# A two-layer encoder trunk: where small constants are fetched, and the order of casts, residual adds and norm operands at the ends of feed-forward and attention

## The chip, the cores and the metric

The kernel runs on one core of a Trainium2 chip. The metric is the device time of one execution in microseconds, the median of several runs. Besides the runs there is one profiled execution, from which all views of the profile come.

The core's engines are named as the profile names them: PE (TensorE, matrix products; PEld is its weight load), DVE (VectorE), ACT (ScalarE), POOL (GpSimd) and SP (SyncE, which here only issues transfers). An engine works through its own queue in order; engines wait for each other by semaphores.

## The reference

Input x has 256 tokens of 1024 float32 values. Each of two layers computes

```
x = x + 1/2 * SwiGLU_1(RMSNorm(x))                     # feed-forward, width 2816
h = RMSNorm(x);  q,k,v = h @ W_in
x = x + concat(windowed_attention_A, differential_attention_B) @ W_out
x = x + 1/2 * SwiGLU_2(RMSNorm(x))
```

and a last RMSNorm gives the output. Every RMSNorm has a learned gain per channel. The attention needs small inputs besides: the gains of the norms, a sink logit per head, four vectors whose products give the lambda of the differential attention, and tables of distances.

## The kernel before

**Precision.** Matrix products are made of three float32r products each. A weight tile lands as `raw` (4 x 128 rows of 512 columns, 1 MB). ACT casts it to `whi`, and DVE subtracts to get the rest, `wlo`. The activations are split in the same way, and each step takes hi x hi, lo x hi and hi x lo. `raw` has 6 buffers, `whi` and `wlo` have 3 each.

**Stream of weights.** All tiles of the whole kernel stand in one list, `specs`, in the order in which they are used. `ahead(n)` (line 198) issues the casts up to tile n and the transfers for which buffers are free; `weights()` (line 219) calls it with two tiles of lookahead and hands out the next tile. The transfers are issued by SP.

**Order of work.** The wrappers `pe`, `act` and `dve` (line 40) keep the program's order while `kept[0]` is true. In `mix`, the attention, it is set to false after the first products (line 780) and to true again before the output projection (line 908); in between a scheduler orders the instructions. POOL is used without a wrapper, so the scheduler may order its instructions throughout.

**A norm** is an instance of `Norm` (line 273). It needs no normalised copy of x: the gain is multiplied into the transposed x, and the row's factor r is applied later to the products.

- `turn(j)` transposes two of eight chunks of x on PE into a bank of PSUM.
- `operands(j)` makes the operand pair j of it. For each of its two chunks, ACT writes gain times x as the high part, and DVE the rest as the low part.
- `squares` sums x squared on ACT. `stats` makes r from the sums, on DVE and POOL.

`make_sums` and `by_seven` belong to another way to multiply, which is off: `SEVEN` is empty, so neither is called.

**Start.** SP fetches the first gain table, and the first tiles of gate and up in four slices of 256 KB each, interleaved; ACT's queue fetches x in four parts. `take_x` (line 381) makes the first norm between the slices: pairs 0 and 1, then 2 and 3, at k == 2 its squares and `stats`. From line 424 on POOL issues eight small transfers of constants (three gain tables, the sinks, the four lambda vectors), the last five broadcast to 128 partitions, then an iota, memsets and small products of them. `attention_constants`, called inside the third column group of the first feed-forward, reads them.

**Feed-forward.** `ffn` goes over five groups of 512 hidden columns and a last one of 256. For each, PE makes gate and up from the norm's operands, ACT and DVE make the hidden values, PE transposes them and adds their product with the down weights into four banks.

**End of a feed-forward** (`ffn_close`, line 688). PE's order is: the products of the last down tiles for the left half of x, written `group(0, ...)`, `tail(0)`; those of the right half, `group(1, ...)` and `tail(1)`, in pieces; between them the transposes for pairs 0 and 1 of the next norm. DVE adds the residual, left half first. The cast of one more weight tile, `ahead(at["use"] + LOOK - 1)`, stands on line 701, behind the pairs and the squares. That tile is the second one used by the next stage. After attention's entry the first products with pairs 0 and 1 run, then `late` makes pairs 2 and 3 from the right half of x.

**End of attention** (from line 841). PE multiplies the values of path B (`osl`, 16 matmuls) and of path A (`oa`, 32 matmuls of 64 columns); the trace has two records for each of these, 32 and 64. `norm_b` (line 858) normalises path B's heads: squares on ACT, sums on DVE, the power on POOL, the product on DVE, eight transposes on PE, and the split with the gain into `oT[2]` and `oT[3]` by ACT and DVE. In the program's text it is called before the last two of the eight (t, c) steps of path A's matmuls. Path A is divided by its sums into `oan` on DVE. Then the output projection runs, first over path B's rows, then over path A's.

Of the kernel before, what the change touches and what calls it, by code (L numbers as in the profile page):

```python
# [34 lines left out]
def trunk(ctx: ExitStack, tc: tile.TileContext, x, n1, g1, u1, d1, nm, w_in, sink,  # L35
          lq1, lk1, lq2, lk2, subln, w_out, n2, g2, u2, d2, nf, out):
    nc = tc.nc
    pool, sp = nc.gpsimd, nc.sync

    class Kept:  # L40


        def __init__(self, eng):
            self.eng = eng
# [26 lines left out]
    def bank():  # L71
        return ps.tile([P, 512], F32, tag="ps", bufs=8, name=nm_("ps"))
# [4 lines left out]
    def blk(dt=F32R):  # L77
        return s4.tile([P, 2, 512], dt, tag="s4", name=nm_("s4"))
# [194 lines left out]
    class Norm:  # L273


        def __init__(self, g0, sums=len(SEVEN) > 0):
            self.g0, self.xs, self.sums = g0, [], sums
            self.xg = []
            self.ss = tmp("nss", 2, (P, 2, 4))

        def squares(self, t, c, n):
# [13 lines left out]
        def operands(self, j, sl):  # L295
            xs = blk()
            self.xs.append(xs)
            for i in range(2):
                g = gcol[:, self.g0 + 2 * j + i:self.g0 + 2 * j + i + 1]
                act.activation(xs[:, i, 0:S], sl[:, i], AF.Identity, scale=g)  # L300
                dve.scalar_tensor_tensor(xs[:, i, S:512], in0=sl[:, i], scalar=g, in1=f(xs[:, i, 0:S]),
                                         op0=ALU.mult, op1=ALU.subtract)
            if self.sums:
                if j % 2 == 0:
                    self.xg.append(blk(F32).rearrange("p a (c s) -> p (a c) s", c=2))
                for i in range(2):
                    act.activation(self.xg[j // 2][:, j % 2 * 2 + i], sl[:, i], AF.Identity,
                                   scale=gcol[:, self.g0 + 2 * j + i:self.g0 + 2 * j + i + 1])

        def make_sums(self):  # L310

            (t0, t1), (b0, b1) = [(t[:, :, 0:P], t[:, :, P:S]) for t in self.xg]
            self.sm = []

            def make(x, y, op):
                v = tmp().rearrange("p a (c s) -> p (a c) s", c=2)
                dve.tensor_tensor(v, x, y, op=op)
# [4 lines left out]
                return v  # L322

            s1 = make(b1, t1, ALU.subtract)
            s2 = make(s1, t0, ALU.add)
            make(t1, t0, ALU.subtract)
            make(b0, s2, ALU.subtract)

        def quarter(self, t, b):

# [50 lines left out]
    def take_x(k):  # L381

        g, u = early
        if k == 0:
            for j in (0, 1):
                sl = norm.turn(j)
                next(g)
                norm.operands(j, sl)
                next(u)
        elif k == 1:  # L390
            for e in (g, u, g, u):
                next(e)
# [12 lines left out]
    grow = const.tile([NG - 16, P], F32, name="grow")  # L405
    distB = const.tile([P, 2, S], F32, name="distB")
# [20 lines left out]
    pool.dma_start(snk_in, sink.rearrange("l h -> (l h)").partition_broadcast(P))  # L427
    for i, a in enumerate((lq1, lk1, lq2, lk2)):
        pool.dma_start(lin[:, i], a.rearrange("l d -> (l d)").partition_broadcast(P))
    pool.iota(dist_i.rearrange("p a b -> p (a b)"), pattern=[[P, 2], [-1, S]], base=0, channel_multiplier=1)  # L430

    for c in range(4):
        pool.memset(qscA[0:64, c:c + 1], -0.125 / slopeA[c])
        pool.memset(qscA[64:128, c:c + 1], -0.125 / slopeA[c + 4])
        pool.memset(qscB[:, c:c + 1], -0.125 / slopeB[c])

    sv = snk_in.rearrange("p (l s c) -> p l c s", l=DEPTH, s=2)
    for t in range(2):
        for l in range(DEPTH):
            pool.tensor_copy(snk[:, l, :, t, :], sv[:, l])  # L440
    pool.tensor_scalar(nsnk.rearrange("p a b c d -> p (a b c d)"), snk.rearrange("p a b c d -> p (a b c d)"),
                       -1.0, 0.0, op0=ALU.mult, op1=ALU.add)
    for i in range(2):
        pool.tensor_tensor(lpr[:, i], lin[:, 2 * i], lin[:, 2 * i + 1], op=ALU.mult)

    def attention_constants():
        gsl = bank()
# [67 lines left out]
    class Residual:  # L515
# [14 lines left out]
        def late(self, k):  # L530

            if k == 1:
                self.nxt.pair(2)
                self.nxt.pair(3)
                self.squares(1)
            elif k == 2:
                self.nxt.stats()
                if self.nxt.sums:
                    self.nxt.make_sums()

    def ffn(norm, aside=None, before=None, final=False):
        def silu(out_, acc, t):
# [95 lines left out]
        tokens(us, norm.xs, weights(), 4)  # L638
        h = hidden(g, us)
        for n in range(1, NGRP):  # L640
            if n == 3 and aside is not None:
# [12 lines left out]
            h = hidden(g, us)  # L654
            for hh in range(2):
                down(hT, n - 1, hh, weights())
# [31 lines left out]
    def ffn_close(parts, nxt):  # L688
        group, tail = ffn_end(parts, (FC - 1, G4 + 3))
        res = Residual(nxt, parts[0])  # L690
        group(1, [(0, t) for t in range(2)])
        tail(0)
        for t in range(2):
            res.add(0, t)
        tail(1)
        group(1, [(1, t) for t in range(2)])
        for j in range(2):
            nxt.pair(j)
        res.squares(0)
        group(1, [(2, t) for t in range(2)])  # L700
        ahead(at["use"] + LOOK - 1)
        group(1, [(3, t) for t in range(2)])
        for t in range(2):
            res.add(1, t)
        nxt.late = res.late

    def mix(l, norm, nxt_norm):
# [150 lines left out]
        def norm_b():  # L858
# [16 lines left out]
            for hp, src in enumerate(turned(on)):  # L875
# [66 lines left out]
    for l in range(DEPTH):  # L942
        final = l == DEPTH - 1
        parts = ffn(norm, attention_constants, take_x) if l == 0 else ffn(norm)
        norm_m = Norm(16 + l * 8, False)
# [77 lines left out]
```

## Time and profile before

| what | value |
|---|---|
| time, median of 3 runs | 976.37 us (976.16 to 978.26) |
| profiled execution, its own time | 975.68 us |
| its span in the profile | 973.9 us |
| instructions | 12341 |
| granted clock of PE, mean | 0.999 |
| PE busy | 956.1 us |
| DVE, ACT, POOL busy | 558.7, 479.0, 20.2 us |
| moved by DMA | 169.38 MB, mean 174 GB/s |

How to read the views. Times run from the span's start. A line in order of time gives the start, the duration, the engine, the line of the code, the operation, what it writes <- what it reads, the shape and how often; in square brackets stands the idle time of the engine before it, and what ended that. Most instructions carry line 50, the wrapper's, so they are told apart by their tiles: `ps` is a bank of PSUM, `s` an operand or hidden block, `ident` the matrix for transposes, `xk` the residual x. A window's line gives its length, the busy time and number of instructions of each engine, the clock and the share of DMA.

### The profile page before, as it was taken

The numbers are of one execution on the slowest core, as the hardware profiler recorded it, in microseconds if no ns is written. First come the engines' busy times: TensorE is split into PE (matmuls) and PEld (weight loads), VectorE is DVE, ScalarE is ACT, GpSimd is POOL, SyncE is SP. The second block draws the span as 40 slices with busy tenths as digits, with TensorE's granted clock in tenths as the row PEclk, the third lists the DMA queues.
The fourth block names the chain that finished last, engine by engine and source line by source line (L and its number), as shares of the span: only waits on it lengthen the run. The fifth ranks groups of instructions, "written<-read, shape, count | busy, mean of one in ns | idle before, by whom it ended". The sixth has DMA issues, their size and how long they took to land.

```text
span 973.9 us, 12341 instructions
## 1 busy us (share of the span) xinstructions
PE 956.1 (98%) x4940; PEld 807.9 (83%) x4940; DVE 558.7 (57%) x854; ACT 479.0 (49%) x781; POOL 20.2 (2%) x49
## 2 busy tenths in 40 slices
PE   8999999999999999999999999999999999999997
PEld 5888888889888888888888888887999788888886
DVE  4745545479846545445465455555796565445553
ACT  4735444368635534444364434435675464434433
POOL 3000000000000000000000000000000000000001
PEclk9999999999999999999999999999999999999999
DMA  9955556545424655556556556554652356565501
GB/s 284 374 200 190 173 176 212 174 147 153 135 66 151 216 199 190 173 180 208 173 173 195 189 183 201 183 173 132 204 156 73 130 173 201 188 204 202 179 1 43
DMA packets 98217, 169.38 MB, mean 174 GB/s; under 512 B 3182, under 2 KB 30896, under 8 KB 98160
## 3 DMA queue, kind: packets, MB, share of 16 engines
q1 hardware_dynamic: 96816, 167.27, 51.8%
q0 software_dynamic: 256, 0.29, 0.4%
q10 hardware_dynamic: 1088, 1.05, 0.3%
q8 instruction: 38, 0.62, 0.3%
q14 instruction: 19, 0.16, 0.0%
HBM read 167.54 MB, written 1.05 MB: 173 GB/s over the span
## 4 chain that ended last, share of the span: by engine, by line
PE 94%; DVE 2%; DMA 1%; ACT 1%; issue 1%; POOLq 0%; POOL 0%; SPq 0%
PE ps L50 94%; DMA raw<-in_ffn_w_gate_dram 1%; DVE s L50 1%; DVE wlo L50 1%; ACT s L50 0%; ACT whi L50 0%; DVE xk L50 0%; DMA xk<-in_x_dram 0%; ACT junk L50 0%; ACT tmp L50 0%; POOLq L1018 0%; POOL rf L968 0%; DVE rf L50 0%; SPq L162 0%
## 5 line engine op out<-in xcount | busy, mean ns | idle before, releaser
L50 PE MATMUL ps<-whi,s 128*128 128x512 f32 (+1 forms) x2316 | 718.3, 391 | 2.8 <-DVE s L50 1.2
L50 DVE TENSOR_TENSOR wlo<-raw,whi 128x1024 fp32r<-128x1024 f32 (+2 forms) x392 | 378.5, 1014 | 229.8 <-ACT whi L50 225.9
L50 PEld LDWEIGHTS ps<-whi,s 128*128 128x128 f32 x2316 | 431.2, 188 | 91.7 <-ACT whi L50 2.3
L50 PE MATMUL ps<-wlo,s 128*128 128x512 f32 x1158 | 450.8, 389 | 0.2 <-DVE wlo L50 0.2
L50 ACT CAST whi<-raw 128x1024 fp32r<-128x1024 f32 (+2 forms) x392 | 323.1, 884 | 244.9 <-PE ps L50 222.0
L50 PEld LDWEIGHTS ps<-wlo,s 128*128 128x128 f32 x1158 | 217.7, 188 | 47.1 <-DVE wlo L50 2.3
L50 PE MATMUL ps<-s,whi 128*128 128x256 f32 x448 | 83.1, 286 | 1.4 <-ACT whi L50 1.4
L50 PEld LDWEIGHTS ps<-s,whi 128*128 128x128 f32 x448 | 70.1, 192 | 2.8 <-ACT whi L50 1.8
L50 ACT CAST s<-ps 128x512 fp32r<-128x512 f32 x48 | 26.0, 589 | 94.2 <-PE ps L50 94.2
L50 DVE TENSOR_TENSOR s<-ps,s 128x512 fp32r<-128x512 f32 x48 | 31.1, 687 | 71.6 <-ACT s L50 71.6
L50 PE MATMUL ps<-s,wlo 128*128 128x256 f32 x224 | 63.5, 284 | 1.5 <-DVE wlo L50 1.5
L50 ACT ACTIVATE tmp<-ps,r 128x512 f32<-128x512 f32 (+1 forms) x48 | 30.8, 654 | 45.6 <-PE ps L50 45.6
L50 DVE SCALAR_TENSOR_TENSOR s<-ps,hr,tmp 128x512 f32<-128x512 f32 (+1 forms) x48 | 32.4, 706 | 31.8 <-PE ps L50 25.4
L50 ACT ACTIVATE s<-ps,gcol 128x256 fp32r<-128x256 f32 x48 | 21.6, 472 | 51.0 <-PE ps L50 33.1
L50 PEld LDWEIGHTS ps<-s,wlo 128*128 128x128 f32 x224 | 42.9, 192 | 1.9 <-DVE wlo L50 1.9
L50 PE MATMUL ps<-ident,s 128*128 128x128 f32 x304 | 39.9, 273 | 0.0
L50 PEld LDWEIGHTS ps<-ident,s 128*128 128x128 f32 x304 | 35.1, 141 | 4.7
L50 DVE SCALAR_TENSOR_TENSOR s<-ps,gcol,s 128x256 fp32r<-128x256 f32 x48 | 22.3, 482 | 28.2 <-ACT s L50 28.2
L50 ACT ACTIVATE s<-s,negm 128x256 f32<-128x256 f32 x64 | 31.9, 500 | 7.4 <-DVE negm L50 7.4
L345 POOL TENSOR_TENSOR r<-ms,mhalf 128x2 f32<-128x2 f32 x6 | 4.2, 702 | 646.1 <-DVE ms L50 646.1
L50 PE MATMUL ps<-ident,xk 128*128 128x128 f32 x96 | 14.5, 288 | 1.9 <-DVE xk L50 1.1
L50 PEld LDWEIGHTS ps<-ident,xk 128*128 128x128 f32 x96 | 11.6, 146 | 4.7 <-DVE xk L50 1.9
(94 smaller groups left out, 274.4 us busy)
## 6 DMA issues: line engine op xcount, KB each, us to landing
raw<-in_ffn_w_down_dram SPq DMA_DIRECT2D x44, 1024.0 KB, 4.9
raw<-in_ffn_w_gate_dram SPq DMA_DIRECT2D x39, 1024.0 KB, 5.0
raw<-in_ffn_w_up_dram SPq DMA_DIRECT2D x39, 1024.0 KB, 5.0
raw<-in_w_in_dram SPq DMA_DIRECT2D x14, 1024.0 KB, 5.0
raw<-in_ffn_w_gate_dram SPq DMA_DIRECT2D x8, 512.0 KB, 3.6
raw<-in_ffn_w_up_dram SPq DMA_DIRECT2D x8, 512.0 KB, 4.6
raw<-in_w_in_dram SPq DMA_DIRECT2D x8, 512.0 KB, 4.5
raw<-in_w_out_dram SPq DMA_DIRECT2D x4, 1024.0 KB, 4.8
```

The source lines that it names most:

```text
L50: ins = issue(*a, **k)
L345: pool.tensor_tensor(self.r, ms, mhalf[:, 0:2], op=ALU.pow)
```

## The change

Five edits:

1. The constants' block becomes a function `constants()`, called in `take_x` at k == 2 behind `stats()`. POOL gets the wrapper, so its program order is kept.
2. In `operands`, both activations are issued first and then both subtractions.
3. In `ffn_close`, the line with `ahead` moves from behind the next norm's pairs and squares to directly behind `tail(1)`.
4. In `mix`, `kept[0] = True` moves up, ahead of path A's matmuls, so that the end of attention, `norm_b` among it, stands in program order.
5. `make_sums` is rewritten and its calls move; as `SEVEN` is empty, it is called neither before nor after.

```diff
-    pe, act, dve = Kept(nc.tensor), Kept(nc.scalar), Kept(nc.vector)
+    pe, act, dve, pool = Kept(nc.tensor), Kept(nc.scalar), Kept(nc.vector), Kept(nc.gpsimd)
...
         def operands(self, j, sl):
             xs = blk()
             self.xs.append(xs)
-            for i in range(2):
-                g = gcol[:, self.g0 + 2 * j + i:self.g0 + 2 * j + i + 1]
+            gs = [gcol[:, self.g0 + 2 * j + i:self.g0 + 2 * j + i + 1] for i in range(2)]
+            for i, g in enumerate(gs):
                 act.activation(xs[:, i, 0:S], sl[:, i], AF.Identity, scale=g)
+            for i, g in enumerate(gs):
                 dve.scalar_tensor_tensor(xs[:, i, S:512], in0=sl[:, i], scalar=g, in1=f(xs[:, i, 0:S]),
                                          op0=ALU.mult, op1=ALU.subtract)
...
             norm.stats()
-            if norm.sums:
-                norm.make_sums()
+            constants()
...
-    for i, g in enumerate((nm, n2)):
-        pool.dma_start(grow[i * 16:(i + 1) * 16], g.rearrange("l (k p) -> (l k) p", p=P))
-    pool.dma_start(grow[32:34], subln)
...
+    def constants():
+        for i, g in enumerate((nm, n2)):
+            pool.dma_start(grow[i * 16:(i + 1) * 16], g.rearrange("l (k p) -> (l k) p", p=P))
+        pool.dma_start(grow[32:34], subln)
+        pool.dma_start(snk_in, sink.rearrange("l h -> (l h)").partition_broadcast(P))
+        for i, a in enumerate((lq1, lk1, lq2, lk2)):
+            pool.dma_start(lin[:, i], a.rearrange("l d -> (l d)").partition_broadcast(P))
+        pool.iota(dist_i.rearrange("p a b -> p (a b)"), pattern=[[P, 2], [-1, S]], base=0, channel_multiplier=1)
...
         tail(1)
+        ahead(at["use"] + LOOK - 1)
         group(1, [(1, t) for t in range(2)])
         for j in range(2):
             nxt.pair(j)
         res.squares(0)
         group(1, [(2, t) for t in range(2)])
-        ahead(at["use"] + LOOK - 1)
         group(1, [(3, t) for t in range(2)])
...
+        kept[0] = True
         oa = [bank() for _ in range(2)]
         for t in range(2):
             for c in range(4):
...
-        kept[0] = True
         w = weights()
```

On the engines' queues the change leaves the number of instructions as it is. On PE, only the eight transposes at each end of attention move: they stand behind 24 of path A's 32 matmuls (48 of 64 records) instead of behind 30, in between the last ones. On DVE at that place, a small instruction of `norm_b` (`dd`) moves behind the sums of squares, and the division of path A (`ra`, `oan`) behind the split of path B. On ACT and DVE at the three ends of `ffn_close`, the two casts and two subtractions of one tile move ahead of the operands of pairs 0 and 1. On POOL, the constants move behind r.

More of the change, by code (lines that the diff above doesn't have):

```diff
@@ L37, in trunk @@
     nc = tc.nc
-    pool, sp = nc.gpsimd, nc.sync
+    sp = nc.sync
     class Kept:
@@ L273, in trunk, with __init__ @@
     class Norm:
-        def __init__(self, g0, sums=len(SEVEN) > 0):
-            self.g0, self.xs, self.sums = g0, [], sums
-            self.xg = []
+        def __init__(self, g0):
+            self.g0, self.xs = g0, []
             self.ss = tmp("nss", 2, (P, 2, 4))
@@ L297, in operands, with make_sums, part, make @@
             self.xs.append(xs)
-            for i in range(2):
-                g = gcol[:, self.g0 + 2 * j + i:self.g0 + 2 * j + i + 1]
+            gs = [gcol[:, self.g0 + 2 * j + i:self.g0 + 2 * j + i + 1] for i in range(2)]
+            for i, g in enumerate(gs):
                 act.activation(xs[:, i, 0:S], sl[:, i], AF.Identity, scale=g)
+            for i, g in enumerate(gs):
                 dve.scalar_tensor_tensor(xs[:, i, S:512], in0=sl[:, i], scalar=g, in1=f(xs[:, i, 0:S]),
                                          op0=ALU.mult, op1=ALU.subtract)
-            if self.sums:
-                if j % 2 == 0:
-                    self.xg.append(blk(F32).rearrange("p a (c s) -> p (a c) s", c=2))
-                for i in range(2):
[L307 to L317, printed above, removed]
+        def make_sums(self):
+            self.sm = []
+            def part(b, t):
+                vs = [f(self.xs[2 * b + i]) for i in range(2)]
+                return [[v[:, :, c + t * P:c + (t + 1) * P] for v in vs] for c in (0, S)]
+            def make(x, y, op, rest):
+                v = tmp().rearrange("p a (c s) -> p (a c) s", c=2)
+                for i in range(2):
+                    vi = v[:, 2 * i:2 * i + 2]
+                    dve.tensor_tensor(vi, x[i], y[i], op=op)
+                    for z, o in rest:
+                        dve.tensor_tensor(vi, vi, z[i], op=o)
                 sm = blk().rearrange("p a (c s) -> p (a c) s", c=2)
@@ L321, in make @@
                 self.sm.append(sm)
[L322 to L327, printed above, removed]
+                return [v[:, 0:2], v[:, 2:4]]
+            add, sub = ALU.add, ALU.subtract
+            (t0h, t0l), (t1h, t1l), (b0h, b0l), (b1h, b1l) = [part(b, t) for b in range(2) for t in range(2)]
+            s1 = make(b1h, t1h, sub, [(b1l, add), (t1l, sub)])
+            s2 = make(s1, t0h, add, [(t0l, add)])
+            make(t1h, t0h, sub, [(t1l, add), (t0l, sub)])
+            make(b0h, s2, sub, [(b0l, add)])
         def quarter(self, t, b):
@@ L423, in trunk @@
     lpr = lams[:, 1, 0:2 * DEPTH * 64].rearrange("p (i d) -> p i d", i=2)
-    for i, g in enumerate((nm, n2)):
-        pool.dma_start(grow[i * 16:(i + 1) * 16], g.rearrange("l (k p) -> (l k) p", p=P))
-    pool.dma_start(grow[32:34], subln)
[L427 to L442, printed above, removed]
@@ L443, in trunk @@
-    for i in range(2):
-        pool.tensor_tensor(lpr[:, i], lin[:, 2 * i], lin[:, 2 * i + 1], op=ALU.mult)
+    def constants():
[6 more added lines that the diff above has]
+        pool.iota(dist_i.rearrange("p a b -> p (a b)"), pattern=[[P, 2], [-1, S]], base=0, channel_multiplier=1)
+        for c in range(4):
+            pool.memset(qscA[0:64, c:c + 1], -0.125 / slopeA[c])
+            pool.memset(qscA[64:128, c:c + 1], -0.125 / slopeA[c + 4])
+            pool.memset(qscB[:, c:c + 1], -0.125 / slopeB[c])
+        sv = snk_in.rearrange("p (l s c) -> p l c s", l=DEPTH, s=2)
+        for t in range(2):
+            for l in range(DEPTH):
+                pool.tensor_copy(snk[:, l, :, t, :], sv[:, l])
+        pool.tensor_scalar(nsnk.rearrange("p a b c d -> p (a b c d)"), snk.rearrange("p a b c d -> p (a b c d)"),
+                           -1.0, 0.0, op0=ALU.mult, op1=ALU.add)
+        for i in range(2):
+            pool.tensor_tensor(lpr[:, i], lin[:, 2 * i], lin[:, 2 * i + 1], op=ALU.mult)
@@ L537, in late @@
                 self.nxt.stats()
-                if self.nxt.sums:
-                    self.nxt.make_sums()
     def ffn(norm, aside=None, before=None, final=False):
@@ L640, in ffn @@
         for n in range(1, NGRP):
+            if n + 1 == min(SEVEN, default=0):
+                norm.make_sums()
             if n == 3 and aside is not None:
@@ L944, in trunk @@
         parts = ffn(norm, attention_constants, take_x) if l == 0 else ffn(norm)
-        norm_m = Norm(16 + l * 8, False)
+        norm_m = Norm(16 + l * 8)
         ffn_close(parts, norm_m)
```

## The prediction

> **What bounds the kernel now.** I read the busy shares first, then the chain that ended last, then PE's busy time in long windows, and last the instructions in order of time where PE was not busy.
>
> ```profile
> PE 956.1 (98%) x4940; PEld 807.9 (83%) x4940; DVE 558.7 (57%) x854; ACT 479.0 (49%) x781; POOL 20.2 (2%) x49
> PE 94%; DVE 2%; DMA 1%; ACT 1%; issue 1%; POOLq 0%; POOL 0%; SPq 0%
> ```
>
> TensorE (PE) is busy for 956.1 of 973.9 us, and 94% of the chain is PE. Only PE's 17.8 idle us can be won. The windows say where they lie (columns: length, then busy us of PE, PEld, DVE, ACT, POOL, then clock and DMA):
>
> ```profile
> 0.00:20.00 20.00, 15.24 (x57) 10.30 (x58) 8.04 (x15) 8.78 (x15) 8.98 (x37) 1.00 0.92 262
> 190.00:210.00 20.00, 18.00 (x121) 16.06 (x121) 9.95 (x20) 10.21 (x22) 0.70 (x1) 1.00 0.51 157
> 270.00:280.00 10.00, 9.06 (x74) 8.43 (x74) 5.28 (x10) 3.16 (x7) 1.64 (x1) 1.00 0.01 2
> 480.00:500.00 20.00, 19.80 (x96) 16.19 (x95) 11.02 (x17) 9.55 (x19) 0.00 (x0) 1.00 0.42 135
> 670.00:690.00 20.00, 18.02 (x127) 16.31 (x126) 10.44 (x21) 10.67 (x23) 0.69 (x1) 1.00 0.42 136
> 750.00:760.00 10.00, 9.06 (x68) 8.19 (x68) 5.72 (x10) 3.33 (x6) 1.52 (x1) 1.00 0.01 2
> 950.00:973.90 23.90, 16.91 (x94) 14.54 (x92) 9.30 (x17) 7.50 (x16) 3.69 (x4) 0.94 0.12 44
> ```
>
> Idle: 4.76 us at the start, 2.00 and 1.98 at the two entries to attention, 0.94 at each end of attention, 0.20 at the entry to layer 1's first feed-forward, 6.99 at the end. Everywhere between, PE is busy the whole window (for instance 170.00 of 170.00 from 20 to 190), so a microsecond won ahead of such a stretch reaches the end if the other engines move with it. The change touches each of these places but the last.
>
> I price each place from start to start of matmuls, because a wait also breaks the pipeline: a matmul of 512 columns starts 0.227 us after the one before (three in 0.68), one of 256 columns 0.12 (three in 0.36), a record of 64 columns 0.111 (60 in 6.65), eight transposes 0.79.
>
> **1. The cast of the second weight tile, moved ahead of the operands (three entries).** Attention of layer 0:
>
> ```profile
> 196.85 0.40 PE L50 MATMUL ps<-s,whi 128*128 128x256 f32 x2
> 198.06 4.06 ACT L50 CAST whi<-raw 128x1024 fp32r<-128x1024 f32 x6
> 199.14 0.50 PE L50 MATMUL ps<-s,whi 128*128 128x256 f32 x2 [0.69 <-ACT whi L50]
> 200.40 0.39 PE L50 MATMUL ps<-s,wlo 128*128 128x256 f32 x1 [0.76 <-DVE wlo L50]
> 202.13 0.33 PE L50 MATMUL ps<-ident,xk 128*128 128x128 f32 x1 [0.28 <-DVE xk L50]
> 203.47 0.49 PE L50 MATMUL ps<-s,whi 128*128 128x256 f32 x2
> ```
>
> PE waits for whi, for wlo, and then for the residual add, which stands on DVE behind wlo. From 196.85 to 203.47 it issues 24 matmuls of 256 columns and 8 transposes: 24 x 0.12 + 0.79 = 3.67 us of work in 6.62.
>
> Moved, the cast waits for a whi buffer: three exist, and this one is read by tail(1), whose matmuls end at 191.9. The tile itself had landed at 164.9 by its semaphore's record, so no DMA holds it. The two casts (2.0) end at 193.9; ACT was idle for 6.8 us there. Queued behind them are the operand activations, which could start at 193.87 anyway. The two wlo (2.36 from 192.9) end at 195.25. Queued behind on DVE are four operand subtractions (0.48 + 3 x 0.40): pair 0 ready at 196.1, pair 1 at 197.0; PE asks for pair 0 at 196.85, so 0.7 us of cover is left. The adds follow (1.28, to 198.3); PE reaches their transposes at 196.85 + 24 x 0.12 = 199.7. All four waits go: 6.62 - 3.67 = **2.95 us**. Layer 1 (675.58 to 682.18): 6.60 - 3.67 = **2.93**. At the entry to layer 1's first feed-forward one triple takes from 491.43 to 492.59 instead of 0.68: **0.48**. Bounds: at least the two weight waits (1.45 a time) at the attention entries and nothing at the third; at most these sums. I take the sums, for each successor is covered. What is late next is nothing on PE: the tile after it had landed at 171.5, too.
>
> **2. Both activations ahead of both subtractions in operands().** Now ACT's second waits for DVE's first and DVE's second for ACT's second (0.55 and 0.54 each time). In the new order ACT waits for neither. Only one place could be on the path, the start; elsewhere PE is busy, so I cost it at nothing, its cover being PE's own stream. The wait it adds: DVE's first subtraction waits for both activations, some 0.2 to 0.4 us, with the next wlo behind it; in part 1 this is counted.
>
> **3. The end of attention in program order.**
>
> ```profile
> 269.38 6.81 PE L50 MATMUL ps<-vA,s 128*128 128x64 f32 x60
> 276.03 0.39 PE L50 MATMUL ps<-ident,s 128*128 128x128 f32 x2
> 277.76 0.50 PE L50 MATMUL ps<-whi,s 128*128 128x512 f32 x1 [0.34 <-ACT s L50]
> 278.87 0.50 PE L50 MATMUL ps<-whi,s 128*128 128x512 f32 x1 [0.60 <-DVE s L50]
> 279.43 0.63 PE L50 MATMUL ps<-whi,s 128*128 128x512 f32 x2
> ```
>
> Now the eight transposes of the normalised heads stand behind 60 of the 64 records of small matmuls, and DVE puts the second half of oan (0.69) ahead of the subtractions that the output projection needs. In the new order the transposes stand behind 48, at 269.38 + 48 x 0.111 = 274.7. Their source is ready at 274.15, or 274.3 with the dd instruction (0.17) that moves in front: a wait is added to PE's queue with 0.4 us of cover, and 16 small records behind it. ACT then scales from 275.2 to 276.5, DVE subtracts from 275.9 to 277.3; PE reaches the projection near 277.3. The oan work, 0.17 + 2 x 0.69, moves behind and ends at 278.8; its reader is PE 24 matmuls (5.4 us) later, and the wlo behind it has a reader two tiles on. From 269.38 to 279.43 are 10.05 us for 64 x 0.111 + 0.79 + 3 x 0.227 = 8.57: **1.48**. Layer 1 (748.09 to 758.14) has the same 10.05. Bounds: the idle 0.94 alone, and 1.48. I take 1.48 twice.
>
> **4. The constants, moved behind the first norm.** POOL's eight DMAs, iota, 12 memsets, four copies and three small operations now follow the r of the first norm; nothing else waits in POOL's queue until the next norm, near 210. SP's queue keeps its order, but shares the 16 DMA engines. In the window from 8 to 14 us (packets, MB, share of the engines):
>
> ```profile
> q0 software_dynamic: 149, 0.26, 61.5%
> q1 hardware_dynamic: 393, 0.73, 38.9%
> ```
>
> The constants' queue q0 moved 0.26 MB and held 61.5% of the engines' time (many of its 4 KB packets took 1.2 to 1.9 us); the weights' q1 got 38.9%, at 168 GB/s in all against 389 from 14 to 20. By the semaphores, the second gate slice landed at 8.14, the next ones at 12.00, 15.08, 16.13, 16.75 and 17.40. Without q0, 1.2 MB remain after 8.0; at 389 GB/s they land at 8.6, 9.3, 9.9, 10.6 and 11.2. What binds then is the second gate slice and PE itself: its wlo comes at 9.51 as now, and from the matmul at 9.54 PE has 40 matmuls and 8 transposes (40 x 0.227 + 0.79 + 0.1) until the next tile's first, at 19.5. That one starts at 21.93 now: **2.4 us**. DVE and ACT hold: the third slice's wlo is ready at 11.1, asked for at 11.8; the whole tile's at 16.2 onward, asked for at 19.5. Bounds: 0.7 (0.26 MB at 389 GB/s) and 3.0 (the second slice 0.5 us sooner as well). I take 2.4.
>
> The Trainium skill, "DMA: Bandwidth & Descriptors", section "Anatomy of one DMA — SWDGE (gpsimd) path", gives a transfer from this queue about 2 us fixed plus its bytes at 436 GB/s; by that 0.26 MB would hold the engines an estimated 0.6 us, this part would give about 0.6 and the whole change 1.8 less. The trace does not agree: 61.5% of 6 us is 3.7.
>
> The work is not gone: POOL will issue near 24 us. At worst the weights behind it fall back to today's landings (33.6, 36.3, 39.0), whose casts began at 39.86, 45.39 and 50.02; the cover of 6.3 us or more shrinks by the 2.4 that PE runs ahead, and stays. The constants are first read near 100 us.
>
> **Sum.** 2.4 + 2.95 + 2.93 + 0.48 + 2 x 1.48 = 11.7 us. The profiled execution took 975.68 (span 973.9), so 964.0; the median of the runs is 0.69 above it, so **964.6 us**, 1.2% faster.
>
> **Rivals.**
> - *The start gives only the constants' bytes.* The slow stretch is then not q0's doing, and the start wins 0.7: 966.3. For: other loads began then too. Against: q1's own packets kept their usual duration, there were only few. 0.10.
> - *DVE takes over in attention.* It is busy 9 tenths in slice 9 (219 to 243). If its chain rather than PE's sets that stage, the 5.9 us of its entries are lost: 970.5. Against: PE had no idle time there from 210 to 270, and DVE's own start (the adds, 201.4) moves forward by over 4 us. 0.08.
> - *Slower: the constants starve the weights later.* Place: near 25 to 40 us. Price: their hold was 17.40 - 11.2 = 6.2 us. PE stalls once the hold passes about 10 us (landing 27.5 against a cast at 37.5) and the kernel is slower than before only beyond 10 + 11.7 us, over three times as long; then 979 or more. 0.03.
> - *The orders do not differ in effect:* every wait has another cause: 976. 0.02.
>
> My forecast has 0.77. Its own range is 963 to 967.5; bounds of several parts met together give 970.9, so the range is 962.5 to 969.5. A measurement of this kernel tells about 0.2% (2 us) from no change. Faster 0.95, same 0.02, slower 0.03.
>
> **What would show it.** PE's waits near 199, 680, 278 and 757 gone; PE busy without a gap from about 9.5 us; q0's packets near 27 to 34 us with no idle PE there; ACT's second activation without a wait on DVE; the last 7 idle us unchanged. Wrong would be: an operand wait of PE at 196.85 (cover 0.7), a wait at the transposes near 274.7 (cover 0.4), or a late third slice at 11.8.

## The result and the profile after

| | before | after |
|---|---|---|
| time, median (lowest to highest) | 976.26 us (975.84 to 978.26, 4 runs) | 964.63 us (964.20 to 965.28, 4 runs) |
| profiled execution, its own time | 975.68 us | 964.2 us |
| its span | 973.9 us | 962.4 us |
| PE idle in the span | 17.8 us | 11.1 us |

The ratio is 0.9875, with a 95% interval of 0.9863 to 0.9888: 1.2% faster. The page of the kernel after, its busy shares and its chain of work that ended last:

```profile
PE 951.3 (99%) x4940; PEld 807.9 (84%) x4940; DVE 557.4 (58%) x854; ACT 478.2 (50%) x781; POOL 20.1 (2%) x49
PE 98%; DMA 0%; issue 0%; DVE 0%; ACT 0%; POOLq 0%; POOL 0%; ACTq 0%; DVEq 0%
```

PE's share of the chain rose from 94 to 98%. The windows of the kernel after, at the places of those shown of before (there the entries and ends stand up to 10 us later):

```profile
0.00:20.00 20.00, 15.97 (x68) 12.57 (x69) 12.43 (x24) 13.76 (x26) 0.90 (x8) 1.00 0.93 329
180.00:200.00 20.00, 20.00 (x119) 17.58 (x118) 13.79 (x21) 11.71 (x23) 0.00 (x0) 1.00 0.59 164
260.00:270.00 10.00, 10.00 (x93) 10.00 (x92) 4.05 (x8) 1.78 (x3) 1.64 (x1) 1.00 0.01 2
470.00:490.00 20.00, 20.00 (x98) 16.68 (x97) 12.39 (x18) 10.85 (x19) 0.00 (x0) 1.00 0.61 205
660.00:680.00 20.00, 20.00 (x141) 18.64 (x140) 11.31 (x24) 10.68 (x24) 0.70 (x1) 1.00 0.50 159
740.00:750.00 10.00, 10.00 (x73) 9.24 (x73) 6.55 (x11) 3.33 (x6) 1.38 (x1) 1.00 0.00 0
940.00:962.40 22.40, 15.33 (x87) 13.23 (x85) 8.38 (x15) 5.92 (x14) 3.69 (x4) 0.89 0.13 47
```

The first number behind the comma is PE's busy time: it fills every window but the first and the last. The tail's idle time is as it was (7.07 us against 6.99). Of 4.76 idle us at the start 4.03 stay, and the view of PE's waits says for what (us in total, times, longest):

```profile
PE ps L50 <- DMA grow<-in_ffn_norm_dram: 3.4, 1, 3.4
PE ps L50 <- DMA xk<-in_x_dram: 0.7, 2, 0.4
```

They are the first gain table and rows of x. The waits for `whi`, `wlo`, `s` and the residual are gone from this list.

At the start, PE's lines in order of time. The first three are of the kernel before: two waits for casts of slices that landed late, and the first matmul with the first whole tile (the expectations below call it the second). The last is that matmul in the kernel after:

```profile
12.69 0.73 PE L50 MATMUL ps<-whi,s 128*128 128x512 f32 x2 [0.57 <-ACT whi L50]
...
15.77 0.73 PE L50 MATMUL ps<-whi,s 128*128 128x512 f32 x2 [0.28 <-ACT whi L50]
...
21.93 0.61 PE L50 MATMUL ps<-whi,s 128*128 128x512 f32 x2
```

```profile
19.52 0.62 PE L50 MATMUL ps<-whi,s 128*128 128x512 f32 x2
```

The entry to attention in layer 0, some of the instructions in order of time, kernel after:

```profile
189.42 2.00 ACT L50 CAST whi<-raw 128x1024 fp32r<-128x1024 f32 x2 [4.80 <-PE ps L50]
...
191.50 1.57 ACT L50 ACTIVATE s<-ps,gcol 128x256 fp32r<-128x256 f32 x4
...
192.78 1.65 DVE L50 SCALAR_TENSOR_TENSOR s<-ps,gcol,s 128x256 fp32r<-128x256 f32 x4
...
194.35 1.28 DVE L50 TENSOR_TENSOR xk<-xk,ps 128x512 f32<-128x512 f32 x2
194.44 0.40 PE L50 MATMUL ps<-s,whi 128*128 128x256 f32 x2
...
197.31 1.03 PE L50 MATMUL ps<-ident,xk 128*128 128x128 f32 x8
198.10 0.48 PE L50 MATMUL ps<-s,whi 128*128 128x256 f32 x2
```

The cast stands ahead of the activations, the eight transposes are one unbroken record, and from the first matmul with pair 0 to the first with pair 2 are 198.10 - 194.44 = 3.66 us, where it was 6.62 and the work was counted as 3.67. The end of attention, kernel after:

```profile
264.01 5.47 PE L50 MATMUL ps<-vA,s 128*128 128x64 f32 x48
269.31 1.04 PE L50 MATMUL ps<-ident,s 128*128 128x128 f32 x8
270.19 1.90 PE L50 MATMUL ps<-vA,s 128*128 128x64 f32 x16
271.90 0.72 PE L50 MATMUL ps<-whi,s 128*128 128x512 f32 x2
...
272.69 0.63 PE L50 MATMUL ps<-whi,s 128*128 128x512 f32 x2
```

No bracket stands on any line, and PE's waits above name none here. From 264.01 to 272.69 are 8.68 us, against 10.05.

Where the time came from, by the same matmul in both traces (start times):

| checkpoint | before | after | ahead by | gained here |
|---|---|---|---|---|
| first whole tile's first matmul | 21.93 | 19.52 | 2.41 | 2.41 |
| transposes at attention's entry, layer 0 | 193.23 | 190.81 | 2.42 | 0.01 |
| first path A matmul | 269.38 | 264.01 | 5.37 | 2.95 |
| fourth product of the output projection | 279.43 | 272.69 | 6.74 | 1.37 |
| layer 1's first feed-forward, behind the triple | 492.59 | 485.38 | 7.21 | 0.47 |
| attention's entry, layer 1, pair 2 | 682.18 | 671.96 | 10.22 | 3.01 |
| fourth product of the output projection | 758.14 | 746.54 | 11.60 | 1.38 |

The fifth row is the entry at which one triple of matmuls had come late. Its line in the kernel before:

```profile
492.25 0.50 PE L50 MATMUL ps<-wlo,s 128*128 128x512 f32 x1 [0.20 <-DVE wlo L50]
```

The span became 11.5 us shorter. What was won at each place stayed won up to the end.

The constants did not vanish. Three windows of the kernel after (last two columns: share of the DMA engines, GB/s):

```profile
8.00:14.00 6.00, 6.00 (x30) 4.51 (x28) 4.88 (x9) 4.61 (x9) 0.00 (x0) 1.00 1.06 393
...
26.00:32.00 6.00, 6.00 (x29) 4.95 (x28) 4.33 (x6) 4.64 (x6) 4.62 (x23) 1.00 1.09 319
32.00:38.00 6.00, 6.00 (x32) 5.08 (x31) 2.94 (x4) 1.89 (x4) 1.27 (x2) 1.00 0.98 259
```

From 8 to 14 us the weights now come at 393 GB/s instead of 168. The hold has moved to about 30 to 35 us, where two neighbouring weight tiles land at 29.87 and 36.01 by the semaphores, 6.14 us apart instead of the 2.7 that is usual, and PE is busy 6.00 of 6.00 us.

### The profile page after: what moved, and what is told of

Same layout as the page of the kernel before. It is cut to its first block, busy times and chain, and to the rows that moved or that the text cites. A ratio compares the mean times of both kernels' runs of the same rounds, so it can differ in the third digit from the quotient of the medians.

```text
span 962.4 us, 12393 instructions
## 1 busy us (share of the span) xinstructions
PE 951.3 (99%) x4940; PEld 807.9 (84%) x4940; DVE 557.4 (58%) x854; ACT 478.2 (50%) x781; POOL 20.1 (2%) x49
## 4 chain that ended last, share of the span: by engine, by line
PE 98%; DMA 0%; issue 0%; DVE 0%; ACT 0%; POOLq 0%; POOL 0%; ACTq 0%; DVEq 0%
PE ps L50 98%; DMA xk<-in_x_dram 0%; DVE s L50 0%; ACT tmp L50 0%; DVE xk L50 0%; POOLq L1022 0%; POOL rf L50 0%; ACTq L50 0%; DVE rf L50 0%; DVEq L50 0%
## 5 line engine op out<-in xcount | busy, mean ns | idle before, releaser
L50 ACT ACTIVATE s<-ps,gcol 128x256 fp32r<-128x256 f32 x48 | 19.3, 473 | 19.1 <-PE ps L50 19.0
L50 DVE SCALAR_TENSOR_TENSOR s<-ps,gcol,s 128x256 fp32r<-128x256 f32 x48 | 20.3, 477 | 12.5 <-ACT s L50 12.4
L50 ACT ACTIVATE junk<-xk 128x512 f32<-128x512 f32 x24 | 15.3, 637 | 0.4
L50 PE MATMUL ps<-vA,s 128*128 128x64 f32 x128 | 14.7, 273 | 0.0
```

The lines of the kernel that those rows point to most:

```text
L50: ins = issue(*a, **k)
```

## The experiments

The theory is that of the prediction: each edit takes away its own waits of PE, and the sum reaches the end. The rivals are that an edit does nothing or that another does its work, and for part 4 that the bytes, the queue or the loads' pattern matter. Each kernel is the changed one with the edit shown, but for `a1`, which is the kernel before. The first four rows shared a chip and its runs of before, as did the next four and the last three; before's medians there were 977.33, 976.09 and 976.76 us. So a difference of under 1 us between kernels of different groups can't be read from the medians; the traces decide there.

| kernel | median, us (range) | ratio to before, 95% | span, us |
|---|---|---|---|
| u1, constants early again | 967.88 (966.29 to 968.43) | 0.9899 [0.9879, 0.9919] | 966.6 |
| u2, cast late again | 968.4 (967.91 to 969.31) | 0.9908 [0.9889, 0.9927] | 966.7 |
| u3, end scheduled again | 967.7 (967.33 to 968.29) | 0.9900 [0.9882, 0.9919] | 966.2 |
| u4, operands by turns again | 964.76 (964.38 to 965.85) | 0.9871 [0.9848, 0.9894] | 963.3 |
| a1, before + constants late | 974.33 (973.28 to 976.18) | 0.9980 [0.9971, 0.9990] | 973.4 |
| a2, only the lambda loads late | 964.18 (964.16 to 965.01) | 0.9879 [0.9865, 0.9892] | 962.4 |
| q1, lambda loads early on SP | 965.7 (965.16 to 966.34) | 0.9893 [0.9879, 0.9906] | 963.0 |
| x3, lambda loads three times | 964.05 (963.70 to 964.35) | 0.9875 [0.9862, 0.9889] | 962.6 |
| w1, u2 and u4 together | 971.65 (970.99 to 972.28) | 0.9946 [0.9930, 0.9963] | 969.2 |
| x9, lambda loads nine times | 966.01 (965.79 to 966.24) | 0.9887 [0.9872, 0.9901] | 964.0 |
| s1, gate slices first | 964.97 (964.39 to 966.08) | 0.9877 [0.9863, 0.9892] | 962.7 |

### u1: the constants early again

```diff
             norm.stats()
-            constants()
...
+    constants()
+
     def attention_constants():
```

> The changed kernel with one part undone: the constants' block is called at its old place, ahead of everything, and no longer behind the first norm's statistics. My theory (the constants' packets hold the DMA engines from 8 to 14 us, and the weight slices wait): the gain of the start is lost, 964.6 + 2.4 = 967.0 us; the second whole tile's first matmul near 21.9 instead of 19.5 us; the third gate slice lands near 15 instead of 10. Rival (the start was won by the order of activations and subtractions): 964.6, no difference.

3.3 us come back, and in its profile 4.2. The hold is back too: from 8 to 14 us all transfers together run at 157 GB/s (packets, MB, share of the engines):

```profile
q0 software_dynamic: 128, 0.25, 58.5%
q1 hardware_dynamic: 367, 0.68, 41.1%
```

The third gate slice landed at 15.73 instead of 10.01, near the 15 expected. Matmuls of u1 in order of time:

```profile
11.68 0.39 PE L50 MATMUL ps<-wlo,s 128*128 128x512 f32 x1
14.39 1.14 PE L50 MATMUL ps<-whi,s 128*128 128x512 f32 x2 [2.32 <-ACT whi L50]
15.33 0.63 PE L50 MATMUL ps<-wlo,s 128*128 128x512 f32 x1
```

The slice ahead of that one, the second of up, landed at 13.70 (9.33 in the changed kernel), and PE waits for its cast. From 11.68 to 14.39 are 2.71 us where matmuls else follow after 0.23, so this accounts for 2.5 us; the rest is in the clock column of two windows (0.76 and 0.50 behind the instruction counts):

```profile
14.00:15.00 1.00, 0.61 (x2) 0.42 (x2) 0.63 (x1) 0.34 (x1) 0.04 (x1) 0.76 0.93 334
15.00:16.00 1.00, 1.00 (x4) 0.79 (x3) 0.07 (x1) 0.25 (x1) 0.00 (x0) 0.50 0.99 383
```

Behind the wait the granted clock is 0.50 from 14.51 to 17.93, and matmuls stand 0.43 us apart instead of 0.227: another 1.7 us. So the first whole tile's first matmul stands at 23.83, not near the 21.9 expected. The early constants' price is a wait, and in some executions half a clock behind it: the fastest of u1's four executions, 966.29 us, has a mean granted clock of 0.999, the others 0.997.

### u2, u4 and w1: the cast and the order of the operands

u2 moves the cast back:

```diff
         tail(1)
-        ahead(at["use"] + LOOK - 1)
...
         group(1, [(2, t) for t in range(2)])
+        ahead(at["use"] + LOOK - 1)
```

> The changed kernel with one part undone: the cast of one more weight tile stands again behind the next norm's pairs and squares. My theory: 2.95 + 2.93 + 0.48 us come back, 971.0 us, with PE's waits for whi, wlo and the residual add at both entries to attention. Rival (the entries were won by the order of the operands, and the place of the cast matters little): 965 to 966, and the waits stay away.

u4 makes the operands by turns:

```diff
             for i, g in enumerate(gs):
                 act.activation(xs[:, i, 0:S], sl[:, i], AF.Identity, scale=g)
-            for i, g in enumerate(gs):
                 dve.scalar_tensor_tensor(...)
```

> The changed kernel with one part undone: activation and subtraction of an operand pair by turns again. The forecast cost this edit at nothing. Worked out again on top of the other parts: with the cast ahead, DVE reaches the four subtractions only near 192.8 us and each second activation then waits for a subtraction, so that the residual adds end about 2 us later and PE waits some 0.4 us at each of the two entries to attention, and about 0.1 at the start: 964.6 + 0.9 = 965.5 us. If it is really worth nothing: 964.6. Rival (the new order is what made the start faster): 967.0.

u4 measured as the changed kernel does: the new order is worth nothing there. Its span is 0.9 us longer, all of it ahead of the third set of transposes at 14.05 us (13.19 after), and most of it is a longer wait for rows of x (the longest 1.4 us, against 0.4). u2 lost 3.8 us, less than the 6.4 expected and more than the rival's 1. Its entry to attention, in order of time:

```profile
192.47 1.57 ACT L50 ACTIVATE s<-ps,gcol 128x256 fp32r<-128x256 f32 x4 [6.88 <-issue]
195.31 4.06 ACT L50 CAST whi<-raw 128x1024 fp32r<-128x1024 f32 x6
...
197.65 0.38 PE L50 MATMUL ps<-s,wlo 128*128 128x256 f32 x1 [0.41 <-DVE wlo L50]
...
199.39 0.33 PE L50 MATMUL ps<-ident,xk 128*128 128x128 f32 x1 [0.28 <-DVE xk L50]
199.98 0.98 PE L50 MATMUL ps<-ident,xk 128*128 128x128 f32 x7 [0.27 <-DVE xk L50]
```

ACT makes its four activations without a pause and reaches the late cast 2.84 us after the first of them. Before, with ACT and DVE waiting for each other by turns, it took 198.06 - 193.87 = 4.19. So PE's waits for `whi` (0.69) and half of that for `wlo` are gone although the cast stands where it stood. That gave the third kernel, with both edits taken back:

> The changed kernel without its parts 1 and 2 together: the cast ahead moved back behind the output group, and the operands made by turns (activation, subtraction, activation, subtraction). Question: why the cast moved back alone gave back only 1.65 us at each entry of attention (transposes to the first matmul of the last heads: 74.85 us against 73.20) and nothing at the feed-forward entry of layer 1 (9.08 us in both), where the prediction had 2.95 and 0.48. Theory I (the two parts cover for each other: with both activations first ACT reaches the late casts 1.30 us sooner, so part 2 alone already saves 1.30 at such an entry and 0.53 at the feed-forward's, and part 1 then adds only 1.65; with part 1 in, part 2 has nothing left to do): all comes back, 76.15 us at each entry of attention and 9.61 at the feed-forward's, 964.6 + 2 x 2.95 + 0.53 = 971.0 and up to 1 us more for the start, which differs by that much from run to run (first x row landed at 5.2 to 6.2 us). Theory II (part 1 is worth 1.65 and the rest of the 2.95 came from elsewhere, so part 2 does nothing with or without it): 968.0 to 968.8, as with the cast moved back alone.

It measured 971.65. Its entry, in order of time, has the waits of before again:

```profile
197.13 0.50 PE L50 MATMUL ps<-s,whi 128*128 128x256 f32 x2 [0.75 <-ACT whi L50]
198.39 0.39 PE L50 MATMUL ps<-s,wlo 128*128 128x256 f32 x1 [0.76 <-DVE wlo L50]
```

The four kernels make a square. In each cell stands the median, then the time from the transposes at attention's entry to the first path A matmul (layer 0), then that from the first set of transposes to the second at the entry to layer 1's first feed-forward:

| | both activations first | by turns |
|---|---|---|
| cast ahead | 964.63; 73.20; 9.08 | 964.76; 73.20; 9.08 |
| cast late | 968.4; 74.85; 9.08 | 971.65; 76.20; 9.59 |

Theory I holds. Each edit hides part of the same waits. The new order alone would save 1.35 of the 3.00 us at an entry and all 0.51 at the feed-forward; the cast alone saves all of both. Together they give 3.00 and 0.51, not the sum.

### u3: the end of attention scheduled again

```diff
-        kept[0] = True
         oa = [bank() for _ in range(2)]
...
+        kept[0] = True
         w = weights()
```

> The changed kernel with one part undone: the end of attention is left to the scheduler again, up to the output projection. My theory: 2 x 1.37 (as the two traces have it; 1.48 was forecast) come back, 967.4 us, the transposes behind 60 of the 64 records. Rival (with the stream already ahead, the projection would not wait): 964.6.

967.7, as expected (+3.1). PE's waits in u3 (total us, times, longest) name the same two at the ends of attention as before:

```profile
PE ps L50 <- DVE s L50: 1.2, 2, 0.6
...
PE ps L50 <- ACT s L50: 0.7, 2, 0.3
```

From the first path A matmul to layer 1's transposes are 215.75 us in u3 and 214.34 in the changed kernel: 1.41 at layer 0's end. From layer 1's first path A matmul to the end of the span are 225.91 and 224.55: 1.36. The remaining 1 us of its span lies at the start.

### a1, a2 and q1: which of the constants, and why

a1 is the kernel before with its constants behind the first norm:

> The kernel before with one part done alone: the constants' block behind the first norm's statistics (POOL in program order). My theory (the parts add up): 976.3 - 2.3 = 974.0 us. Rival (the start needs the new order of the operands as well): under 1 us won, 975.5 or more.

974.33, 1.8 us faster than its runs of before (976.09). In its profile the entry to attention comes 2.14 us earlier, but there the clock halves, from 200.76 to 204.17, behind the waits that this kernel still has. A window of a1 (the clock is 0.50):

```profile
202.00:203.00 1.00, 1.00 (x7) 1.00 (x6) 1.00 (x3) 0.00 (x0) 0.00 (x0) 0.50 1.07 414
```

So the time from there to the first path A matmul is 77.76 us instead of 76.15, and 1.6 us of the gain are lost again in this execution. Among executions with a mean granted clock of 0.998 or more, the medians are 973.8 us in a1 (5 of 11) and 975.9 in its kernel before (10 of 15): 2.1 us.

a2 fetches the constants early again, except the four lambda vectors:

```diff
-            constants()
+            lambdas()
...
+    constants()
```

Here `constants()` no longer holds the four loads and the two products of them; `lambdas()` does.

> The changed kernel, but only the four lambda vectors' loads and their products stay behind the statistics; the gain tables, the sinks, the iota and the rest are issued early again. My theory: the hold comes from the lambda loads alone, whose 64 packets of 4 KB lasted up to 2 us each: 964.6 to 965.0 us, and the weight slices land as in the changed kernel. Rival (eight transfers of POOL's queue as such, or POOL's work, hold the start): 966 or more.

964.18, the same as with all of them late. From 8 to 14 us its weights come at 388 GB/s. So the four loads of 64 KB are the hold, and neither the number of transfers nor POOL's queue as such.

q1 takes these four loads from POOL and issues them early, on SP behind the slices:

```diff
+    for i, a in enumerate((lq1, lk1, lq2, lk2)):
+        sp.dma_start(lin[:, i], a.rearrange("l d -> (l d)").partition_broadcast(P))
```

> The changed kernel, but the four lambda loads are issued by SP, early, right behind the eight weight slices; the other constants stay behind the statistics. Theory P (the slow packets come of the source, one row of 512 B read for 128 partitions): packets again last over 1 us, the tile behind them lands 4 to 6 us later, near 19 us, and PE waits about 1 to 2 us for it: 965.5 to 966.5 us. Theory Q (they come of POOL's queue): packets of ordinary duration, under 0.3 us, the tile lands within 1 us of its time in the changed kernel: 964.6 us.

965.7, and the four loads delay SP's queue too. A window of q1 in which nearly nothing but these loads was in flight:

```profile
12.00:14.00 2.00, 2.00 (x13) 1.71 (x12) 1.49 (x3) 0.68 (x2) 0.00 (x0) 1.00 0.21 59
```

The engines moved 59 GB/s and were busy for 0.21 of the time. The first whole tile, behind these loads in the same queue, landed at 19.19 instead of 14.75, 4.4 us late, and the way from the third transposes to attention's entry took 0.6 us more (178.23 against 177.62): the first matmuls with that tile, from 19.89 on, stand 0.33 to 0.39 us apart instead of 0.227. The time and the landing are as theory P had them, but its signs are not. PE's waits name no cast and no tile, and the packets are not slow: in q1 the loads go in packets of 512 bytes, of about 0.03 us each, where POOL's queue has 4-KB packets of up to 2 us that fill the engines. So the delay of the tile follows the loads to another queue, but on SP the tile stands behind them in the same queue while the engines are mostly idle. Each load reads one row of 512 bytes for 128 partitions; whether it is the same address, the small source or something else that makes them slow was not tried. All four executions of q1 (965.16 us and more) took longer than all four of a2 (up to 965.01), on the same chip, but by little: the medians differ by 1.5 us.

### x3 and x9: how long a hold the start can stand

```diff
+        for h in range(2):
+            for i, a in enumerate((lq1, lk1, lq2, lk2)):
+                pool.dma_start(spare[:, h, i], a.rearrange("l d -> (l d)").partition_broadcast(P))
```

In x9 this is done for four spare blocks. Nothing reads them.

> The changed kernel with the four lambda loads issued three times behind the statistics, twice into a block that nobody reads: the hold on the weights is tripled, from about 6 to about 18 us. As the forecast had it (PE stalls once the hold passes about 10 us, the cover being the time to the cast): 7 us slower than the changed kernel, about 971.5. Rival, worked out since (PE uses a tile only some 8 us after its cast could begin, so the cover is about 18 us): 964.6 to 965.5, and the constants could be much longer without any cost.

> The changed kernel with each of the four loads of the lambda vectors made nine times, eight of them into blocks that nothing reads: a probe of how long a hold of the weights the start can stand. With three of each the whole tile that was issued at 26.88 us landed at 49.83, 8.4 us later than in the changed kernel, for eight more loads, 1.05 us each, and its cast began at 53.70 with PE never waiting. From that trace a tile's cast begins two tiles of 5.44 us before PE needs it, so a landing has until about 62 us. Theory (the hold grows by 1.05 us a load, and the cover ends there, not at the 10 us that the prediction took): 32 more loads put that landing at 41.4 + 33.6 = 75 us, PE waits for it some 11 to 13 us, and the time is 975 to 978 us. Rival (SP's packets take turns with the small ones, so a longer list does not hold the weights any longer): the landing stays before 62 us, no wait, 964.6. A middle result, 966 to 973, would say that the loads spread and part of the weights pass between them.

Both forecasts of a stall fell; x9's time is at the foot of the middle result, in which part of the weights pass. In x3 the tile that landed at 41.43 in the changed kernel landed at 49.83, all traffic ran at 103 GB/s from 38 to 44 us, and PE never waited: 964.05. In x9 the hold lasts to 86 us. Two windows of x9, in the hold and where it ends, and the two lines in which PE waits:

```profile
68.00:74.00 6.00, 6.00 (x32) 5.08 (x31) 3.63 (x4) 2.90 (x4) 2.26 (x5) 1.00 0.86 104
...
84.00:90.00 6.00, 5.02 (x21) 3.54 (x20) 2.20 (x2) 2.58 (x3) 0.00 (x0) 1.00 0.93 355
```

```profile
87.82 0.73 PE L50 MATMUL ps<-whi,s 128*128 128x512 f32 x2 [0.46 <-ACT whi L50]
89.08 0.50 PE L50 MATMUL ps<-wlo,s 128*128 128x512 f32 x1 [0.53 <-DVE wlo L50]
```

The weights pass between the small packets, one tile in 7 to 10 us instead of 2.7 (landings 53.33, 60.86, 67.72, 77.78, 86.64). Only the fifth of these tiles is late for PE, though it lands 33.9 us behind the changed kernel's 52.74. Six `raw` buffers, each of which lasts PE 5.44 us, are an estimated 33 us of cover, and that fits. x9 is 1.4 us slower than the changed kernel, not 11 to 13.

### s1: an attempt at a faster start

```diff
-        for e in early:
-            next(e)
+        for e in ((0, 0), (1, 1), (0, 1), (0, 1))[j]:
+            next(early[e])
```

The operands are then taken in that order.

> The changed kernel with another order of the first eight slices on the queue SP: the two gate slices of the first half ahead of the up slices, and the operands taken in that order. It is meant to beat both kernels. In the changed kernel the first matmuls wait for slices that land at 4.68, 6.83, 8.01 and 9.33 us, and the second whole tile's first matmul starts at 19.52. Theory (the start is bound by when the second gate slice lands, which comes about 1.2 us sooner): that matmul starts near 19.05, 964.1 us. Rival (PE's first 2.5 us, in which matmuls of 512 columns come 0.43 us apart, and the rows of x bound the start): no change, 964.4 to 965. The start differs by up to 1 us between runs of one kernel, so a gain of 0.5 us may stay unproved.

The second gate slice landed at 7.00 instead of 8.01, and the time did not change (964.97). The likely reason, which no run tests alone, stands in s1's matmuls:

```profile
9.02 0.94 PE L50 MATMUL ps<-whi,s 128*128 128x512 f32 x2
9.80 0.40 PE L50 MATMUL ps<-wlo,s 128*128 128x512 f32 x1
...
13.45 1.03 PE L50 MATMUL ps<-ident,xk 128*128 128x128 f32 x8
```

Up to 9.45 its matmuls stand 0.43 us apart (in the changed kernel up to 8.51), and the transposes come at 13.45, 0.26 later than there. No kernel tried here was shown to beat the changed one.

## Why the prediction was right, and where it was not

- **What bounds the kernel.** Right: every gain is kept to the end, as the table of checkpoints shows. But "Only PE's 17.8 idle us can be won" is too narrow. Idle time fell by 6.7 us and PE's busy time by 4.8, for the same 4940 matmuls, since matmuls around a wait follow each other more slowly (behind the wait at 12.69 us of the kernel before 0.34 to 0.39 us apart instead of 0.227). The forecast came out because it priced each place from start to start, which holds both. The rival "DVE takes over in attention" is gone: the lead was 5.37 us at attention's first path A matmul and 5.37 behind the entry. So is the one that the orders have no effect: the waits are gone, and come back in w1 and u3.
- **Part 1, 2.95, 2.93 and 0.48.** Right in size: 2.95, 3.01 and 0.47. The weak cover of 0.7 us held, for there is no operand wait at 194.44, and the late triple is gone. But the gain is credited too narrowly, because part 2 could have earned 1.35 of each 3.00 and the whole of the third by itself.
- **Part 2, nothing.** The number holds, since part 1 leaves it no wait to remove. The reason does not: "elsewhere PE is busy" fails at the two places where PE stood still for ACT's late cast, which the order of the operands brings 1.35 us forward. The expectation for u2 took over the same error and was 2.6 us too high.
- **Part 3, 1.48 twice.** The mechanism was right, the term a little large: 1.37 and 1.38 in the traces, 1.41 and 1.36 by u3. The work takes 8.68 us, not 8.57: the transposes with the change of shape around them take 0.88 rather than 0.79, and the first triple behind the small matmuls 0.79 rather than 0.68. The 0.4 us of cover at the transposes sufficed.
- **Part 4, 2.4.** Right in the pair of profiles, 2.41, and the first whole tile's first matmul stands at 19.52, foretold at 19.5. So near a hit is in part luck: in u2, u3, u4 and x3 the same matmul stands at 20.18 to 20.50. By the medians the part is worth 1.8 us in a1 and 3.3 in u1; by executions without a drop of the clock, as far as their mean clock tells, 2.1 and (one execution) 1.7. The rival "only the constants' bytes" (0.7) is out by the 393 GB/s, and a2 shows which of the constants hold the weights. The estimate of 0.6 us for the hold, worked out from the Trainium skill, "DMA: Bandwidth & Descriptors", section "Anatomy of one DMA — SWDGE (gpsimd) path", does not agree with these runs: in u1 the constants' queue holds the engines for 58.5% of 6 us, 3.5 us, in x3 eight more such loads make a tile land 8.4 us later, and part 4 by its profiles gave four times the 0.6.
- **The later cover.** Its outcome was right: the two down tiles behind the moved constants land at 36.01 and 38.73, at the 36.3 and 39.0 of before, and PE does not wait. The threshold was wrong by more than a factor of three. "PE stalls once the hold passes about 10 us" counted from one tile's landing to that tile's own cast. PE needs the cast two tiles later, and behind stand six buffers. The rival built on it, slower than before beyond a hold of 10 + 11.7 us, was therefore even less likely than its 0.03: in x9 a hold of over 50 us (30 to 86), during which part of the weights passed, cost 1.4.
- **The sum.** 11.7 against 11.5 in the profiles; the terms of part 3 are the difference (0.2). That the median came within 0.1 us of 964.6 is luck as well, with a start that varies by up to 1 us.

## What to carry to other kernels

Price two edits at one wait as one, and look what each does without the other, for the second may find nothing left. Count the cover of a late transfer over all buffers of the stream up to the moment when the consumer needs the tile, not up to the next step. Fetch what is read late after the first data are through, above all loads of one small row to all partitions. Their 0.26 MB would take 0.7 us at 389 GB/s; the tile behind them came 4.4 us late on SP (q1), and the last slice 5.35 us late on POOL's queue (17.40 against 12.05).

## What the runs showed of the hardware that was not expected

**A wait can cost twice.** Behind u1's wait of 2.3 us, and behind a1's four waits at 197 to 200.6 us (none over 0.8), the granted clock fell to 0.50 for 3.41 us, which cost 1.7 and 1.6 us more. The profiles of before and of w1 have the waits of a1 at the same place and no such drop, so it does not follow each time. The times without a profile point the same way. Of 29 executions of the kernel before that ran beside these kernels, 15 have a mean granted clock of 0.998 or 0.999 and spans of 973.5 to 974.9 us, the other 14 have 0.996 or 0.997 and 975.0 to 978.6. Of 24 of the changed kernel, u4, a2, q1, x3 and s1, all but one have 0.998 or more. So the medians of before, and with them the ratios above, hold some of this second cost; no profile shows where it fell. The Trainium skill, "TensorE: Matmul & The Clock Gate", section "What's actually happening", says that TensorE's clock is halved or freed by its activity in free-running windows of about 3.4 us; the 3.41 us agree.

**The start is slow for a varying time.** The first matmuls of 512 columns stand 0.43 us apart, later ones 0.227. The trace's record of a clock of 1.0 begins at 7.7 us (u1), 8.6 (before and after), 9.7 (s1) and up to 10.7 (u2, x3); the column shows 1.00 ahead of it too, but the spacing tells. Two us at half pace are 1 us of work. Attention's entry came at 190.81 in the changed kernel and at 191.47 to 191.80 in u2, u3, u4 and x3, whose start has the same edits but for the order in u4. In x3 nearly all of the difference arises from 9.0 to 10.6 us, in this way. In u3 a slice that landed 0.7 us later (8.73 against 8.01) has a part in it, and in u2 and u4 0.6 and 0.8 us stand ahead of that, where PE waits longer for rows of x. So the start varies by the landings as well. The same section of the Trainium skill says that the moment of the change of pace differs from run to run; the runs agree. A change at the start under 1 us can't be read from one profile.
